# Two small scale tables share one tile, and a pin on the second projection stays for the first tile only

## The chip, the cores and the metric

The kernel runs on one core of a Trainium2 chip. The metric is the device time of one execution in microseconds (us). The five engines are called PE (TensorE, matmuls; its weight loads are listed apart as PEld), DVE (VectorE), ACT (ScalarE), POOL (GpSimd) and SP (SyncE, which here only issues DMAs). Each has its own queue of instructions and works it off in order; they wait for one another with semaphores.

## The reference

Two layers of a decoder trunk over 1024 positions of width 1024, all in float32. A layer normalises its input, projects it once to 1312 columns, and gives the columns to three mixers: attention over a sliding window of 128, a pooling mixer, and latent attention over all earlier positions. The mixers' outputs go through one output projection and are added to the residual stream; then comes a gated feed-forward part of inner width 2816.

```
for l in range(DEPTH):
    h = rms_norm(x, attn_norm[l])
    proj = h @ w_in[l]
    ...
    mixed = jnp.concatenate([out_a, out_b, out_c], axis=-1)
    x = x + mixed @ w_out[l]
    h = rms_norm(x, ffn_norm[l])
    x = x + (jax.nn.silu(h @ w_gate[l]) * (h @ w_up[l])) @ w_down[l]
```

## The kernel before, in words

**Numbers.** Every matmul operand is split into two parts, `hi` (rounded to the matmul's type) and `lo` (the rest), with a copy on ACT and a subtraction on DVE (`split`, L57 and L58). A product is then three matmuls: hi with hi, hi with lo, lo with hi. They are the triples of lines L445 to L447, L879 to L881, L1079 to L1081 and L1232 to L1234. In `te.matmul(acc, a, b)` the second argument is the stationary tile (128 columns, loaded as weights), the third the moving one (512 columns wide in most cases).

**Stages.** For each layer: `phase1` (projection, sliding window, pooling), `phase2` (latent attention, output projection), and `phase34`, which is the feed-forward part: `gate_up` and then `down`.

- `phase1` loops over 8 tiles of 128 positions. Per tile, `group0` projects to the first 512 columns (weights `wa` against the transposed input `hT`), then come `proj(512, 512)` (weights `wb`) and `proj(1024, 288)`. Each has 8 triples. What comes out is evacuated on ACT, scaled, and goes into attention. A scheduler puts the instructions of all engines in order by a modelled timeline when the program is built; `tc.issue_after(i)` holds it from placing the instructions in its block before instruction `i`. `G["mm"]` is the last matmul that `proj` made. So the line `with tc.issue_after(G["mm"].ins): acc = proj(512, 512)` pins the second projection of every tile behind the last matmul of the first.
- `gate_up` works on the weights in 44 stages in all (2 layers, 11 pairs of inner columns, gate and up). A stage is a product of 2 x 2 blocks with 7 block products instead of 8. Each block product (`prod`, L1228) is 4 triples, 12 matmuls, so a stage has 84. Moving tiles are the seven blocks of the transposed input, `T1` to `T4`, `B11`, `B21`, `B22`, which stay for the whole stage; stationary are the weights, split into tiles `A11`, `A12` and `sb`. The sums of blocks are made on POOL. Results of a pair are multiplied, split into `go` and stored to DRAM (`gd`).
- `down` does the same for the last projection in 4 chunks of 7 products (L1079 to L1081): stationary is `ga`, loaded from `gd`, moving is `op`, split from the loaded weights `rw`. 1848 matmuls in both layers.

**Memory.** Tiles are placed by pools on two stacks, one that grows up from the low end (left, the default) and one that grows down from the high end (`side="right"`). The first pool of the left stack, `cst`, holds small constants and the residual `xm`, and what is allocated later stands on top of it. Each tile takes a multiple of 32 bytes per partition. In `gate_up`, `T2`, `T3`, the weights as loaded (`raw4`), `A11`, `A12`, `sb` and part of `go` are on the left; `T1`, `T4`, `B11`, `B21`, `B22` are on the right. In `down`, `ga`, the accumulators and the weights of chunks 2 to 4 (`rw`) are on the left, `op` and the first chunk's `rw` on the right.

The start of each tile, in bytes modulo 512, as the program before is built (the parts of a tile that one matmul reads lie multiples of 512 bytes apart, so they start alike):

| part | left stack | right stack |
|---|---|---|
| gate_up | T2, T3, raw4, A11, A12, sb, left go: 0 | T1, T4, B11, B21, B22, right go: 480 |
| down | ga, rw of chunks 2 to 4: 0 | op, rw of chunk 1: 480 |
| phase 1 | hT: 480; wa: 96; wb: 480, 352, 224 or 96 | |
| output projection | moving 0, 128 or 256 on stationary 256; moving 128 on 128 | |

The tables of the change, `gq` and `gm`, are scale vectors of two columns. `gq` is read at L483 and L484 (scale of the queries), `gm` is written in `Boot.bias` and read in phase 2.

Of the kernel before, what the change touches and what calls it, by code (L numbers as in the profile page):

```python
# [11 lines left out]
F32 = mybir.dt.float32  # L12
# [9 lines left out]
P = 128  # L22
# [7 lines left out]
DEPTH = 2  # L30
# [5 lines left out]
@with_exitstack  # L36
def trunk(ctx: ExitStack, tc: tile.TileContext, A, out):
    nc = tc.nc
    ve, sc, gp, te, sy = nc.vector, nc.scalar, nc.gpsimd, nc.tensor, nc.sync

    def pool(stack, name, bufs=1, space=None, side=None):
        kw = {}
        if space is not None:
            kw["space"] = space
        if side is not None:
            kw["side"] = side
        if space != DRAM:
            kw["reuse_waits"] = "tile"
        return stack.enter_context(tc.tile_pool(name=name, bufs=bufs, **kw))

    def gap(stack, name, n, side=None):
        nc.gpsimd.memset(pool(stack, name, side=side).tile([P, n // 4], F32, name="gap")[:, 0:1], 0.0)

    def f(ap):
        return ap.bitcast(F32)

    def split(hi, lo, src):  # L57
        return sc.copy(hi, src), ve.tensor_tensor(out=lo, in0=src, in1=f(hi), op=ALU.subtract)  # L58

    def mm3(dst, terms, first=True, last=True):  # L60
        n = len(terms)
        for i, (a, b) in enumerate(terms):
            te.matmul(dst, a, b, start=first and i == 0, stop=last and i == n - 1)

    def bcast(row, n):
        return row.unsqueeze(0).to_broadcast([P, n])


    cst = pool(ctx, "cst")
    dram = pool(ctx, "dram", space=DRAM)  # L70

    ident = cst.tile([P, P], F32, name="ident")
    nhalf = cst.tile([P, 32], F32, name="nhalf")
    gp.memset(nhalf, -0.5)
    cmask = cst.tile([P, P], F32R, name="cmask")
    identr = cst.tile([P, P], F32R, name="identr")
    invc = cst.tile([P, 2, 16], F32, name="invc")
    sinks = cst.tile([P, DEPTH, 6], F32, name="sinks")
    gna = cst.tile([P, DEPTH * KT], F32, name="gna")
    gqk = cst.tile([P, 4], F32, name="gqk")  # L80
    gains = cst.tile([P, 14], F32, name="gains")
    pscale = gains[:, 0:4].rearrange("p (l k) -> p l k", l=DEPTH)
    gc = [[gains[:, 4 + 2 * l : 5 + 2 * l], gains[:, 5 + 2 * l : 6 + 2 * l], gains[:, 8 + l : 9 + l]] for l in range(DEPTH)]
    gq = cst.tile([P, DEPTH], F32, name="gq")
    gm = cst.tile([P, DEPTH], F32, name="gm")
    cosT = cst.tile([P, NT, 16], F32, name="cosT")
    sinT = cst.tile([P, NT, 16], F32, name="sinT")
    krr = cst.tile([P, NT, 32], F32, name="krr")
    rc = cst.tile([P, NT, 2], F32, name="rc")
    g32 = [cst.tile([P, 32], F32, name=f"g32{l}") for l in range(DEPTH)]  # L90
    rn = cst.tile([P, NT], F32, name="rn")
    xm = cst.tile([P, NT, KT, P], F32, name="xm")
    xrow = [xm[:, t].rearrange("p k c -> p (k c)") for t in range(NT)]

    xres = dram.tile([S, D], F32, name="xres")
    xp = [[dram.tile([P, D], F32, name=f"xp{l}{t}") for t in range(NT)] for l in range(DEPTH)]
    bias_keep = dram.tile([P, 6, 256], F32, name="biask")


    for l in range(DEPTH):  # L100
        xsrc = A["x"][0] if l == 0 else xres
        G = dict(
            ident=ident, xm=xm, xrow=xrow, krr=krr, rc=rc, cosT=cosT, sinT=sinT, sinks=sinks,
            pscale=pscale, invc=invc, nhalf=nhalf, gq=gq, gm=gm, cmask=cmask, identr=identr, rn=rn, gc=gc, g32=g32, xsrc=xsrc, dram=dram, gap=gap, xp=xp, gns=ExitStack(), bias_keep=bias_keep)
        G["gna"], G["gains"], G["gqk"] = gna, gains, gqk
        phase1(nc, tc, A, l, pool, split, f, bcast, G)
        phase2(nc, tc, A, l, pool, split, f, bcast, G)
        phase34(nc, tc, A, l, pool, split, f, bcast, G, xres, out)
# [217 lines left out]
def phase1(nc, tc, A, l, pool, split, f, bcast, G):  # L326
# [3 lines left out]
    with ExitStack() as ph:  # L330
# [104 lines left out]
        for t in range(NT):  # L435
# [5 lines left out]
            def proj(c0, n, hT=hT):  # L441
                acc = ps_mm.tile([P, 512], F32, name="acc")
                for k in range(KT):
                    hi, lo = wcol(0, k, c0, n), wcol(1, k, c0, n)
                    te.matmul(acc[:, 0:n], hT[:, 0, k], hi, start=k == 0, stop=False)  # L445
                    te.matmul(acc[:, 0:n], hT[:, 0, k], lo, start=False, stop=False)  # L446
                    G["mm"] = te.matmul(acc[:, 0:n], hT[:, 1, k], hi, start=False, stop=k == KT - 1)  # L447
                return acc
# [3 lines left out]
            def group0(t):  # L452
                acc = proj(0, 512, hTs[t])
                qk = evq.tile([P, 512], F32, name="qk")
                behind.append(sc.activation(qk, acc, AF.Copy, scale=rows[t]))
                sq = evq.tile([P, 8, 64], F32, name="sq")
                sc.activation(sq.rearrange("p a b -> p (a b)"), qk, AF.Square, scale=0.125)
                ms8 = three.tile([P, 8], F32, name="ms8")
                ve.tensor_reduce(ms8, sq, AX.X, ALU.add)
                return qk, rstd_of(nc, ms8, 8, G["nhalf"])  # L460
# [34 lines left out]

            if l == 0 and t == 0:
                ahead[1] = group0(1)
            with tc.issue_after(G["mm"].ins):
                acc = proj(512, 512)
            vt = three.tile([P, 2, 2, 64], F32R, name="vt")  # L500
            vsrc = acc[:, 0:128].rearrange("p (g d) -> p g d", g=2)
# [476 lines left out]
def phase34(nc, tc, A, l, pool, split, f, bcast, G, xres, out):  # L978
    ve, sc, gp, te, sy = nc.vector, nc.scalar, nc.gpsimd, nc.tensor, nc.sync
    ident, xm, xrow, xp = G["ident"], G["xm"], G["xrow"], G["xp"][l]  # L980
    last = l == DEPTH - 1
    HB = S // 2
    HK = KT // 2
    gd = [[G["dram"].tile([P, 2, HB], F32, name=f"gd{l}_{i}_{p}") for p in range(7)] for i in range(NF // 2)]

    with ExitStack() as ph:
        ps_gu = pool(ph, f"p4gu_{l}", bufs=5, space=PSUM)
        ps_d = pool(ph, f"p4dn_{l}", bufs=3, space=PSUM)
        gate_up(nc, tc, A, l, pool, split, f, bcast, G, ps_gu, ps_d, gd)
        G["gns"].close()  # L990

        down(nc, tc, A, l, pool, split, f, G, (ps_gu, ps_d), gd, xres, out)
# [391 lines left out]
```

## Time and profile before

| | us |
|---|---|
| median of three runs | 2220.33 (2215.66 to 2223.3) |
| the profiled execution | 2220.96 |
| its span in the trace | 2219.2 |
| PE busy in the span | 2142.4 |
| DVE busy | 1690.1 |
| ACT busy | 1088.0 |
| POOL busy | 979.7 |

By the timeline, layer 0 is in phase 1 until about 185 us, in phase 2 until about 440, in gate_up until 888 and in down until 1107; layer 1 follows with 1108, 1291, 1543 and 1996, and ends at 2214. The phases overlap somewhat at their edges.

How to read the rows: a group of the page reads line, engine, operation, out<-in, shapes and count, then busy time and the mean of one in ns, then the engine's idle time before these instructions and who ended it. Matmuls overlap, so what one costs is the distance between two starts on the timeline (start, duration, engine, line, operation). A window's row has the busy time of each engine in it, the granted clock of PE, the share of time that the DMA engines are busy, and GB/s.

### The profile page before, as it was taken

What the parts mean: (1) busy time and instruction counts of PE and PEld (TensorE: products, weight loads), DVE (VectorE), ACT (ScalarE), POOL (GpSimd) and SP (SyncE); (2) the same over time, 40 slices, a digit from 0 to 9 for tenths busy, and PEclk for the clock granted to TensorE, in tenths of its full rate; (3) what the DMA queues carried; (4) which work ended last, traced back from release to release, by engine and by line L of the source; (5) the groups of instructions that cost most, each with busy time, mean ns of one, the idle gap of its engine ahead of it and who ended that gap; (6) DMA issues with size and microseconds to landing.
All of it is one profiled execution on the core that took longest, in us unless ns stands there. A gap on an engine that the chain in (4) does not pass through costs nothing.

```text
span 2219.2 us, 29675 instructions
## 1 busy us (share of the span) xinstructions
PE 2142.4 (97%) x10423; PEld 1766.2 (80%) x10423; DVE 1690.1 (76%) x2595; ACT 1088.0 (49%) x2301; POOL 979.7 (44%) x916
## 2 busy tenths in 40 slices
PE   8998999999999999999989989999999999999999
PEld 6886888877888888788778868888778888887887
DVE  6667888799887887765745688888988878877657
ACT  7777676563434333311356776666534343333111
POOL 2434455255454442621623455452554544436215
PEclk9999999999999999999999999999999999999999
DMA  6003211424434345965520032113244344359754
GB/s 210 1 1 109 83 59 46 134 69 161 166 131 158 136 149 211 417 262 194 200 79 1 1 107 79 67 43 135 76 153 164 138 152 144 143 217 415 265 192 161
DMA packets 133732, 312.16 MB, mean 141 GB/s; under 512 B 13071, under 2 KB 63952, under 8 KB 133584
## 3 DMA queue, kind: packets, MB, share of 16 engines
q1 hardware_dynamic: 133396, 310.19, 38.8%
q8 instruction: 83, 1.36, 0.2%
q14 instruction: 65, 0.53, 0.1%
q10 hardware_dynamic: 188, 0.08, 0.0%
HBM read 203.53 MB, written 106.70 MB: 140 GB/s over the span
## 4 chain that ended last, share of the span: by engine, by line
PE 77%; DVE 9%; DMA 5%; ACT 4%; POOL 3%; issue 2%; SPq 0%; DVEq 0%; POOLq 0%; ACTq 0%
PE gu L1232 11%; PE gu L1234 11%; PE gu L1233 11%; PE dn L1079 6%; PE dn L1080 6%; PE dn L1081 6%; PE acc L445 3%; PE acc L447 3%; PE acc L446 3%; PE tp L840 2%; DMA rw<-in_w_down_dram 2%; PE po L881 1%; PE po L880 1%; PE po L879 1%; PE ss L816 1%
## 5 line engine op out<-in xcount | busy, mean ns | idle before, releaser
L1234 PE MATMUL gu<-T,sb 128*128 128x512 f32 x704 | 277.9, 395 | 6.4 <-DVE sb L58 6.3
L1232 PE MATMUL gu<-T,sb 128*128 128x512 f32 x704 | 278.9, 396 | 3.1 <-ACT sb L58 1.5
L1233 PE MATMUL gu<-T,sb 128*128 128x512 f32 x704 | 278.2, 395 | 0.0
L1079 PE MATMUL dn<-op,ga 128*128 128x512 f32 x616 | 243.7, 397 | 4.8 <-DMA ga<-gd 4.8
L1080 PE MATMUL dn<-op,ga 128*128 128x512 f32 x616 | 244.2, 396 | 0.0
L1081 PE MATMUL dn<-op,ga 128*128 128x512 f32 x616 | 243.4, 396 | 0.0
L1028 POOL TENSOR_TENSOR rw<-rw 128x1536 f32<-128x1536 f32 (+1 forms) x32 | 113.0, 3543 | 254.8 <-DVE op L1038 162.5
L58 ACT CAST go<-xm 128x512 fp32r<-128x512 f32 x154 | 95.2, 620 | 265.2 <-POOL xm L1266 91.5
L1037 ACT CAST op<-rw 128x1536 fp32r<-128x1536 f32 (+1 forms) x56 | 76.7, 1373 | 280.7 <-PE dn L1081 273.1
L1209 POOL TENSOR_TENSOR xm<-raw 128x512 f32<-128x512 f32 x44 | 69.0, 1569 | 324.7 <-DMA raw<-in_w_up_dram 155.1
L58 DVE TENSOR_TENSOR go<-xm,go 128x512 fp32r<-128x512 f32 x154 | 152.9, 1002 | 40.8 <-ACT go L58 37.0
L58 ACT CAST sb<-raw 128x512 fp32r<-128x512 f32 x180 | 110.4, 617 | 133.4 <-PE gu L1234 111.6
L1234 PEld LDWEIGHTS gu<-T,sb 128*128 128x128 f32 x704 | 132.9, 189 | 39.8 <-DVE sb L58 9.3
L1232 PEld LDWEIGHTS gu<-T,sb 128*128 128x128 f32 x704 | 132.8, 189 | 36.6 <-ACT sb L58 3.3
L58 DVE TENSOR_TENSOR sb<-raw,sb 128x512 fp32r<-128x512 f32 x180 | 157.3, 875 | 1.3 <-ACT sb L58 0.3
L1233 PEld LDWEIGHTS gu<-T,sb 128*128 128x128 f32 x704 | 132.9, 189 | 30.2
L1266 POOL TENSOR_TENSOR xm<-xm 128x512 f32<-128x512 f32 x88 | 141.6, 1617 | 31.0 <-DVE go L58 19.6
L1079 PEld LDWEIGHTS dn<-op,ga 128*128 128x128 f32 x616 | 116.1, 188 | 33.7 <-ACT op L1037 5.6
L1038 DVE TENSOR_TENSOR op<-rw,op 128x1536 fp32r<-128x1536 f32 (+1 forms) x56 | 112.0, 2000 | 39.4 <-ACT op L1037 37.1
L1080 PEld LDWEIGHTS dn<-op,ga 128*128 128x128 f32 x616 | 116.2, 189 | 28.1
L1081 PEld LDWEIGHTS dn<-op,ga 128*128 128x128 f32 x616 | 116.2, 189 | 28.0
L1232 PE MATMUL gu<-B,A 128*128 128x512 f32 x336 | 134.5, 400 | 2.8 <-ACT B L58 2.3
(332 smaller groups left out, 6106.1 us busy)
## 6 DMA issues: line engine op xcount, KB each, us to landing
gd<-go SPq DMA_DIRECT2D x154, 512.0 KB, 3.1
ga<-gd SPq DMA_DIRECT2D x154, 512.0 KB, 5.7
raw<-in_w_gate_dram SPq DMA_DIRECT2D x22, 1024.0 KB, 5.4
raw<-in_w_up_dram SPq DMA_DIRECT2D x22, 1024.0 KB, 6.1
rw<-in_w_down_dram SPq DMA_DIRECT2D x44, 512.0 KB, 8.2
xp<-xt SPq DMA_DIRECT2D x32, 256.0 KB, 2.0
old<-xp SPq DMA_DIRECT2D x16, 512.0 KB, 4.2
xp<-xm SPq DMA_DIRECT2D x16, 512.0 KB, 2.9
```

The lines of the kernel that those rows point to most:

```text
L58: return sc.copy(hi, src), ve.tensor_tensor(out=lo, in0=src, in1=f(hi), op=ALU.subtract)
L1028: gp.tensor_tensor(out=o, in0=a, in1=b, op=ALU.subtract)
L1037: sc.copy(t[:, 0], q[b])
L1038: ve.tensor_tensor(out=t[:, 1], in0=q[b], in1=f(t[:, 0]), op=ALU.subtract)
L1079: te.matmul(acc, S_[:, j, 0, ts], T_[:, 0, j], start=j == 0, stop=False)
L1080: te.matmul(acc, S_[:, j, 0, ts], T_[:, 1, j], start=False, stop=False)
L1081: te.matmul(acc, S_[:, j, 1, ts], T_[:, 0, j], start=False, stop=j == h - 1)
L1209: gp.tensor_tensor(out=s1, in0=q["A21"], in1=q["A22"], op=ALU.add)
L1232: te.matmul(acc, s[:, 0, k], b[:, 0, k], start=k == 0, stop=False)
L1233: te.matmul(acc, s[:, 0, k], b[:, 1, k], start=False, stop=False)
L1234: te.matmul(acc, s[:, 1, k], b[:, 0, k], start=False, stop=k == HK - 1)
L1266: gp.tensor_tensor(out=q[o], in0=q[a], in1=q[b], op=op)
```

## The change

Two edits. The two tables become the halves of one tile, so `cst` has one tile less. And the pin on the second projection is kept for the first tile of layer 0 only; for the other 15 tiles the scheduler may place that projection's matmuls where it likes.

```diff
-    gq = cst.tile([P, DEPTH], F32, name="gq")
-    gm = cst.tile([P, DEPTH], F32, name="gm")
+    gqm = cst.tile([P, 2 * DEPTH], F32, name="gqm")
+    gq, gm = gqm[:, 0:DEPTH], gqm[:, DEPTH : 2 * DEPTH]
...
-            with tc.issue_after(G["mm"].ins):
+            with tc.issue_after(G["mm"].ins) if l == 0 and t == 0 else nullcontext():
                 acc = proj(512, 512)
```

The first edit takes one slot of 32 bytes out of the left stack. Everything allocated behind it on the left moves down by 32 bytes per partition; the right stack stays. Modulo 512, the left tiles of gate_up and down go from 0 to 480, so that in both all moving and all stationary tiles start at 480. In phases 1 and 2 all these tiles are on the left, and those of a matmul move together (hT to 448, wa to 64, wb to 448, 320, 192 or 64); the identity matrix, allocated ahead of the tables, stays at 128.

The second edit changes the order of instructions in phase 1 and, in its wake, at the beginning of phase 2. In gate_up and down PE has the same order as before; on SP a few loads and stores of down change places.

The first place is PE in layer 0, tile 2, with `wa` the weights of the first projection and `wb` those of the second. Before, where the first projection ends:

```order
L445 MATMUL acc<-wa_193,hT 128x512
L446 MATMUL acc<-wa_201,hT 128x512
L447 MATMUL acc<-wa_193,hT 128x512
L445 MATMUL acc<-wb_170,hT 128x512
L446 MATMUL acc<-wb_178,hT 128x512
L447 MATMUL acc<-wb_170,hT 128x512
```

After, from the second projection's fourth triple on (buffer numbers are one lower, since there is one tile less):

```order
L445 MATMUL acc<-wb_172,hT 128x512
L446 MATMUL acc<-wb_180,hT 128x512
L447 MATMUL acc<-wb_172,hT 128x512
L445 MATMUL acc<-wa_189,hT 128x512
L446 MATMUL acc<-wa_197,hT 128x512
L445 MATMUL acc<-wb_173,hT 128x512
L446 MATMUL acc<-wb_181,hT 128x512
L447 MATMUL acc<-wa_189,hT 128x512
```

Before, all 24 matmuls of the first projection stand ahead of the second. After, 12 of them do, then 12 of the second follow, and then the two mix: 14 matmuls of the second projection now stand ahead of the last one of the first.

The second place is PE in layer 1, tile 0, where the second projection (512 wide) begins and the third (288 wide) is next. Before:

```order
L445 MATMUL acc<-wb_10684,hT 128x512
L446 MATMUL acc<-wb_10692,hT 128x512
L447 MATMUL acc<-wb_10684,hT 128x512
L445 MATMUL acc<-wb_10685,hT 128x512
L446 MATMUL acc<-wb_10693,hT 128x512
L447 MATMUL acc<-wb_10685,hT 128x512
```

After, from the second triple on:

```order
L445 MATMUL acc<-wb_10684,hT 128x512
L446 MATMUL acc<-wb_10692,hT 128x512
L447 MATMUL acc<-wb_10684,hT 128x512
L445 MATMUL acc<-wb_10683,hT 128x288
L446 MATMUL acc<-wb_10691,hT 128x288
L447 MATMUL acc<-wb_10683,hT 128x288
```

Before, the second projection runs through all its eight triples ahead of the third. After, the third starts behind two triples of the second, and from there they take turns.

## The prediction

> **What bounds the kernel now.** I read the page first, then windows of busy time by stage, then the timeline of TensorE (PE) inside one feed-forward stage.
>
> ```profile
> span 2219.2 us, 29675 instructions
> PE 2142.4 (97%) x10423; PEld 1766.2 (80%) x10423; DVE 1690.1 (76%) x2595; ACT 1088.0 (49%) x2301; POOL 979.7 (44%) x916
> PE 77%; DVE 9%; DMA 5%; ACT 4%; POOL 3%; issue 2%; SPq 0%; DVEq 0%; POOLq 0%; ACTq 0%
> L1234 PE MATMUL gu<-T,sb 128*128 128x512 f32 x704 | 277.9, 395 | 6.4 <-DVE sb L58 6.3
> L1079 PE MATMUL dn<-op,ga 128*128 128x512 f32 x616 | 243.7, 397 | 4.8 <-DMA ga<-gd 4.8
> ```
>
> PE is busy for 97% and carries 77% of the chain that ended last. Its mean per matmul (395 ns) overlaps the next matmul, so the cost of one is the distance between two starts. The windows (us, busy time of PE, weight load, DVE, ACT, POOL, then granted clock, DMA share, GB/s) show where PE is full:
>
> ```profile
> 0.00:185.00 185.00, 170.40 (x941) 143.84 (x942) 118.12 (x262) 139.05 (x367) 60.91 (x153) 0.98 0.25 80
> 442.00:500.00 58.00, 54.13 (x242) 42.51 (x241) 54.49 (x73) 35.23 (x65) 33.19 (x24) 0.97 0.23 75
> 500.00:880.00 380.00, 378.04 (x1623) 305.68 (x1622) 312.87 (x382) 150.72 (x261) 177.07 (x113) 1.00 0.43 153
> 1543.00:1600.00 57.00, 53.23 (x255) 41.52 (x255) 51.18 (x75) 39.51 (x75) 26.49 (x20) 1.00 0.29 95
> ```
>
> From 500 to 880 us PE is busy for 378.04 of 380 and DVE for 312.87: only a faster matmul shortens this. Whether one can be faster is seen in one stage, the start of the first matmul of each block of 12 (T2, T1, T3, B22, T4, B11, B21, and T2 of the next stage), with two rows inside the first:
>
> ```profile
> 620.42 0.39 PE L1232 MATMUL gu<-T,sb 128*128 128x512 f32 x1
> 621.58 0.39 PE L1234 MATMUL gu<-T,sb 128*128 128x512 f32 x1
> 622.94 0.39 PE L1234 MATMUL gu<-T,sb 128*128 128x512 f32 x1
> 623.16 0.40 PE L1232 MATMUL gu<-T,sb 128*128 128x512 f32 x1
> 625.97 0.39 PE L1232 MATMUL gu<-T,sb 128*128 128x512 f32 x1
> 628.71 0.40 PE L1232 MATMUL gu<-B,sb 128*128 128x512 f32 x1
> 631.51 0.40 PE L1232 MATMUL gu<-T,sb 128*128 128x512 f32 x1
> 634.31 0.40 PE L1232 MATMUL gu<-B,A 128*128 128x512 f32 x1
> 637.11 0.40 PE L1232 MATMUL gu<-B,A 128*128 128x512 f32 x1
> 639.91 0.39 PE L1232 MATMUL gu<-T,sb 128*128 128x512 f32 x1
> ```
>
> The blocks with T2 and T3 as moving tile take 2.74 us (620.42 to 623.16, 625.97 to 628.71), the other five 2.80 or 2.81. Inside T2 the first five steps take 1.16 us (232 ns each, still the slow pace), the six from 621.58 to 622.94 take 1.36 (226.7 ns each). The same instruction with the same stationary tile settles at 226.7 or stays at 2.80/12 = 233.3. T2 and T3 are the two moving tiles that lie in the left stack, at 0 modulo 512, where the stationary tiles lie too; the other five lie in the right stack, at 480.
>
> **The change, part by part.**
>
> *The shared tile.* No instruction goes; the readers of gq and gm wait for what they waited for. Everything behind the tile on the left moves down by 32 bytes: T2, T3 and all stationary tiles of gate_up and down go from 0 to 480, the right stack stays at 480. So every pair in the feed-forward part agrees. The price of agreement is 226.7 ns a matmul if address is the cause. Two places outside test that: in the output projection the moving tile lies at 0 for the matmuls from 439.30 and at 128 for those from 440.43, the stationary one at 256.
>
> ```profile
> 439.30 0.39 PE L880 MATMUL ss<-wot,ch 128*128 128x512 f32 x1
> 440.43 0.40 PE L879 MATMUL ss<-wot,ch 128*128 128x512 f32 x1
> 441.12 0.49 PE L1155 MATMUL tp<-ident,xm 128*128 128x128 f32 x3
> ```
>
> Five steps at (0, 256) take 1.13 us, 226 each; three at (128, 256) take 0.69, 230 each. In phase 1 the pair is (480, 480) for the three matmuls on the first wb tile (the start of the fourth closes them):
>
> ```profile
> 96.81 0.39 PE L445 MATMUL acc<-wb,hT 128*128 128x512 f32 x1
> 97.50 0.40 PE L445 MATMUL acc<-wb,hT 128*128 128x512 f32 x1
> 1227.31 0.39 PE L445 MATMUL acc<-wb,hT 128*128 128x512 f32 x1
> 1227.76 0.39 PE L447 MATMUL acc<-wb,hT 128*128 128x512 f32 x1
> 1227.99 0.40 PE L445 MATMUL acc<-wb,hT 128*128 128x512 f32 x1
> ```
>
> They take 0.69 and 0.68 us, and the last step of the second set 0.23 (1227.76 to 1227.99): compatible with 226.7, too short a run to settle. I read the rows as: what counts is that the two starts agree modulo 256.
>
> Gate_up: a stage of 84 matmuls takes 639.91 − 620.42 = 19.49 us; at 226.7 throughout, 19.04. That is 0.45 us; 2 layers x 11 x (gate, up) = 44 stages give **−19.8**. Down has 3 x 616 = 1848 matmuls (the L1079 row and its two sisters), all at 480 against 0:
>
> ```profile
> 957.65 0.40 PE L1079 MATMUL dn<-op,ga 128*128 128x512 f32 x1
> 964.65 0.40 PE L1079 MATMUL dn<-op,ga 128*128 128x512 f32 x1
> ```
>
> 30 steps in 7.00 us are 233.3 each; 1848 x 6.6 ns is **−12.2**. Together −32.0.
>
> The Trainium skill speaks against this in "SBUF — State Buffer", section "Who interferes with whom": PE reads the moving tile and the weights through two independent ports, so the relation of their addresses should cost nothing, and these 32.0 would be 0. The trace disagrees, 2.74 against 2.80 us for equal blocks.
>
> What takes some back: at the entry of each feed-forward part DVE, not PE, sets the pace (54.49 busy of 58, 51.18 of 57). There a faster PE only waits longer: (242 + 255) matmuls x 5.4 ns (0.45/84) = **+2.7**.
>
> *The hand-over to down.* Here transfers bind. The window, the DMA view of 880 to 945 us and the row of the wait:
>
> ```profile
> 888.00:940.00 52.00, 49.65 (x207) 39.61 (x206) 37.72 (x33) 18.93 (x26) 30.82 (x13) 0.97 1.03 417
> GB/s 406 418 408 424 424 416 424 416 413 401 368 418 421 406 418 429 411 426 418 413 429 413 426 418 418 421 418 426 413 426 418 413 431 398 426 418 416 424 416 426
> ga<-gd SPq DMA_DIRECT2D x23, 512.0 KB, 9.9
> 918.24 0.47 PE L1079 MATMUL dn<-op,ga 128*128 128x512 f32 x1 [2.35 <-DMA ga<-gd]
> ```
>
> At 918.24 PE has waited 2.35 us for ga; the group's 4.8 for the whole run says that layer 1 has as long a wait. Transfers are full (share 1.03), so a PE that comes sooner waits longer: 918.24 − 888 is 30 us, 30/0.2333 x 6.6 ns = 0.8 us a layer that isn't won. Second, ga, the left half of go and the later weights now land at 480 instead of 0 modulo 512. No row prices that: the mean of 417 already mixes tiles at both places. Bounds: nothing (rate as now), or the lowest slice, 368, over the 38 us of full transfers that the view shows before the wait (880 to 918): 38 x (417/368 − 1) = 5.1. I take the lower of the ordinary slices, 406: 38 x (417/406 − 1) = 1.0, since most slices lie within 3% although tiles at 480 are among them. So 1.8 a layer, **+3.6** (bounds 1.6 to 11.8). On SP's queue in down one store of go, one reload of the residual rows and three loads of weights change places with a few ga loads, all behind the wait at 918, and each layer takes roughly the order that the other has now; as both wait 2.4, I cost it at nothing, and were that cover gone it is one ga landing more, 9.9 us at full queues, inside the range's upper end for one layer. The Trainium skill bears on it in "DMA: Bandwidth & Descriptors", section "How a descriptor splits into AXI transactions": an access that does not start on a 256-byte boundary fetches from the boundary below. A 4096-byte row at 480 starts 224 past one and would take 135 beats for 128, an estimate of 5.5% or 2.1 us a layer in place of 1.0; no run here shows it yet.
>
> *The order in phase 1.* Without the pin, the second projection of most tiles mixes with the first, or the third. With the matmuls move their evacuations on ACT and DVE and the small power instructions on POOL; no DMA is issued by them. Nothing is added; whom it serves changes. PE waits there for this:
>
> ```profile
> PE acc L445 <- ACT hT L58: 6.2, 6, 1.4
> PE tp L616 <- DVE pT L58: 5.9, 1, 5.9
> ```
>
> (1108 to 1291 us, and 0 to 185.) At best the 6.2 us for hT are filled; at worst the first projection ends 14 matmuls later (3.3 us) before its qk chain, and one more wait like the 5.9 opens. PE idles for 14.6 us of the first window, so later work has cover in both directions: I take **0** (−6.2 to +5.9).
>
> The profiled execution took 2220.96 us (span 2219.2 and 1.8 around it), 0.6 above the median of 2220.33, so I use its own time. Sum: 2220.96 − 32.0 + 2.7 + 3.6 + 0 = 2195.3, **2195 us**.
>
> **Rivals.**
>
> *Half of it.* Agreement buys the faster pace only where a block has settled, and the steady change of stationary tiles, or DVE's casts, unsettles it again. For: the five slow steps at the start of T2. Against: those follow a block that disagrees, and 226.7 then holds across six weight loads. Half of the gain: 2220.96 − 16.0 + 1.4 + 3.6 = 2210.
>
> *The addresses are not the cause, but the ends of the memory.* Fast blocks have both tiles in the left stack, slow ones one on each side. Then nothing changes in the feed-forward part, and only slower landings remain: 2220.96 + 2 x 1.0 = 2223. The rule of the Trainium skill's "SBUF — State Buffer" above, that the two reads never meet, would give this too. Against: the wa tiles (96) and hT (480) are both on the left, and still
>
> ```profile
> 68.33 0.40 PE L445 MATMUL acc<-wa,hT 128*128 128x512 f32 x1
> 70.42 0.28 PE L597 MATMUL s<-kr,qs 128*128 128x256 f32 x1
> ```
>
> nine of them take 2.09 us, 232 each.
>
> *Slower: a moving tile at 480 is slow by itself.* All 4488 matmuls that stay at 233.3 (5 blocks x 12 x 44, and 1848 of down) have their moving tile at 480; the settled runs shown have it at 0. Then T2 and T3 lose what they have: 2 blocks in each of 44 stages, 2.80 − 2.74 = 0.06 us a block, +5.3; the other blocks and down gain nothing, and landings add 2.0: 2220.96 + 7.3 = 2228, with the upper bound of landings (2 x 5.1) 2236. It decides as soon as a T2 block takes over 2.78 us. For: no long run at (480, 480) exists in this trace. Against: the two triples at 1227 and 97 us, and the (128, 256) matmuls, which a good place of the moving tile alone would let settle.
>
> **How the numbers follow.** Forecast 0.76; half 0.08; nothing 0.05; slower 0.11. The forecast's own range is 2184 (no loss at the entries, transfers at 1.6, phase 1 at −6.2) to 2204 (transfers at 11.8). The half case at 2210 is taken in: 2184 to 2212 leaves out the last two cases, 0.16, and little more. About 0.3% (6.7 us) is what a measurement of this kernel can tell from no change. Faster: 0.76 and most of the half case, 0.83. Same: nothing, and the edges of half and slower, 0.07. Slower: 0.10.
>
> **What would show it.** Right: all seven blocks of a stage at 2.72 us, a stage at 19.04 to 19.1; 30 steps of down in 6.80; the wait for ga at the hand-over grown from 2.35 to about 4.2; DVE's share in gate_up up by some 2%. Wrong: T2 blocks at 2.80 (slower), T1 blocks still at 2.80 (nothing), blocks between 2.75 and 2.78 (half); a wait for ga over 8.3 us (2.35 + 5.9) (landings dearer than my bound); PE's idle time before 185 us or between 1108 and 1291 moved by over 6 us (the order mattered).

## The result, and the profile after

The changed kernel takes 2192.48 us (median of 4 runs, 2191.64 to 2196.21) against 2221.55 for the kernel before (4 runs): ratio 0.9877, 95% interval 0.9855 to 0.9899, so about 27 us or 1.2% faster (the two medians lie 29 apart). The profiled execution took 2191.85 us, its span 2190.0, 29.2 less than the span before. Run again with the last experiments the ratio was 0.9878 (0.9858 to 0.9899).

The page of the changed kernel:

```profile
span 2190.0 us, 29669 instructions
PE 2106.4 (96%) x10423; PEld 1762.0 (80%) x10423; DVE 1696.8 (77%) x2595; ACT 1083.7 (49%) x2301; POOL 972.0 (44%) x916
L1234 PE MATMUL gu<-T,sb 128*128 128x512 f32 x704 | 276.1, 393 | 7.5 <-DVE sb L58 7.4
L1079 PE MATMUL dn<-op,ga 128*128 128x512 f32 x616 | 240.5, 392 | 8.1 <-DMA ga<-gd 6.9
```

The count of matmuls is the same, PE's busy time is 36 us less. The waits behind it grew: for `sb` from 6.3 to 7.4 us, for `ga` from 4.8 to 6.9. Note how little the mean of one (393 against 395 ns) shows: it contains the overlap with the next matmul. The starts show the change. One stage of gate_up, the first matmul of each block (T2, T1, T3, B22, T4, B11, B21, next T2):

```profile
617.48 0.39 PE L1232 MATMUL gu<-T,sb 128*128 128x512 f32 x1
620.20 0.39 PE L1232 MATMUL gu<-T,sb 128*128 128x512 f32 x1
622.92 0.39 PE L1232 MATMUL gu<-T,sb 128*128 128x512 f32 x1
625.64 0.39 PE L1232 MATMUL gu<-B,sb 128*128 128x512 f32 x1
628.36 0.39 PE L1232 MATMUL gu<-T,sb 128*128 128x512 f32 x1
631.08 0.39 PE L1232 MATMUL gu<-B,A 128*128 128x512 f32 x1
633.80 0.39 PE L1232 MATMUL gu<-B,A 128*128 128x512 f32 x1
636.52 0.39 PE L1232 MATMUL gu<-T,sb 128*128 128x512 f32 x1
```

Every block takes 2.72 us, the stage 19.04 instead of 19.49, as forecast. In down, 34 steps between two starts of the same line take 7.71 us, 226.8 ns each:

```profile
950.13 0.39 PE L1079 MATMUL dn<-op,ga 128*128 128x512 f32 x1
957.84 0.39 PE L1079 MATMUL dn<-op,ga 128*128 128x512 f32 x1
```

Two windows of the changed kernel, the entry of the first feed-forward part and its steady stretch:

```profile
442.00:500.00 58.00, 53.39 (x242) 42.46 (x241) 54.24 (x72) 34.38 (x64) 33.21 (x24) 0.97 0.23 75
500.00:880.00 380.00, 377.48 (x1655) 311.17 (x1654) 324.10 (x387) 151.43 (x264) 178.38 (x113) 1.00 0.45 160
```

In the first, PE issues 242 matmuls in 58 us, as many as before: there the faster step gains nothing, DVE (54.24 busy) sets the pace, as the prediction had it. In the second it issues 1655 instead of 1623, 2.0% more in the same time, and DVE's busy time rises with it (312.87 to 324.10).

Where the time went, by the start of PE's first instruction of each phase (us, from the timeline; gate_up begins with its first transpose, L1155, and the last column ends with the last matmul's start):

| kernel | layer 0: phases 1, 2 | gate_up | down | layer 1: phases 1, 2 | gate_up | down |
|---|---|---|---|---|---|---|
| before | 429.5 | 453.5 | 222.1 | 433.2 | 453.2 | 218.1 |
| after | 428.5 | 446.1 | 218.8 | 427.1 | 444.8 | 214.8 |
| after, run again | 431.8 | 446.3 | 218.7 | 424.3 | 445.6 | 215.4 |

Before to after (unrounded), gate_up gives 15.7 us, down 6.7, phases 1 and 2 give 7.2, of which 6.2 in layer 1.

These times scatter between executions of one kernel, and the traces show one reason. The granted clock of PE is either full or one half, and the halves come in pieces of 3.41 us, or two or three in a row. At half clock equal matmuls start 427 ns apart (rows below), so a piece in which PE is busy costs 1.7 us. Layer 1's phases 1 and 2 had 30.7 us at half clock in one profile of the changed kernel, 20.5 in the other and 27.3 in the profile before. Where the text says "at full clock", half of such time is taken off: an estimate, since PE is not busy throughout.

### The profile page after: what moved, and what is told of

Same layout as the page of the kernel before. It is cut to its first block, busy times and chain, and to the rows that moved or that the text cites. A ratio compares the mean times of both kernels' runs of the same rounds, so it can differ in the third digit from the quotient of the medians.

```text
span 2190.0 us, 29669 instructions
## 1 busy us (share of the span) xinstructions
PE 2106.4 (96%) x10423; PEld 1762.0 (80%) x10423; DVE 1696.8 (77%) x2595; ACT 1083.7 (49%) x2301; POOL 972.0 (44%) x916
## 3 DMA queue, kind: packets, MB, share of 16 engines
q8 instruction: 83, 1.36, 0.3%
## 4 chain that ended last, share of the span: by engine, by line
PE 48%; DVE 6%; DMA 4%; ACT 2%; issue 1%; POOL 1%; SPq 0%; DVEq 0%; ACTq 0%; POOLq 0%
PE gu L1234 6%; PE gu L1233 6%; PE gu L1232 6%; PE dn L1079 5%; PE dn L1081 5%; PE dn L1080 5%; PE acc L445 2%; PE acc L446 2%; PE acc L447 2%; DMA ga<-gd 1%; PE tp L840 1%; DMA raw<-in_w_up_dram 1%; PE po L881 1%; PE po L879 1%; DVE xm L1069 1%
## 5 line engine op out<-in xcount | busy, mean ns | idle before, releaser
L1079 PE MATMUL dn<-op,ga 128*128 128x512 f32 x616 | 240.5, 392 | 8.1 <-DMA ga<-gd 6.9
L1080 PE MATMUL dn<-op,ga 128*128 128x512 f32 x616 | 240.7, 391 | 0.0
L1081 PE MATMUL dn<-op,ga 128*128 128x512 f32 x616 | 240.0, 391 | 0.0
```

The lines of the kernel that those rows point to most:

```text
L1079: te.matmul(acc, S_[:, j, 0, ts], T_[:, 0, j], start=j == 0, stop=False)
L1080: te.matmul(acc, S_[:, j, 0, ts], T_[:, 1, j], start=False, stop=False)
L1081: te.matmul(acc, S_[:, j, 1, ts], T_[:, 0, j], start=False, stop=j == h - 1)
```

## The experiments

The theory after the result: the shared tile gives about 22 us, all in the feed-forward part, because moving and stationary tiles then agree modulo 256 bytes; the new order gives about 7 us in phase 1. Rivals: everything comes from the addresses (phase 1 moved by 32 bytes as well); agreement modulo 512 is needed; it matters at which place the tiles lie; landings at 480 cost transfers. Each kernel was timed against the kernel before on the same chip.

**The shared tile alone.**

```diff
-            with tc.issue_after(G["mm"].ins) if l == 0 and t == 0 else nullcontext():
+            with tc.issue_after(G["mm"].ins):
```

(against the changed kernel)

> The shared tile alone, with the pin on the second projection of every tile as before; each engine has the order of the kernel before. Theory (address and order add up): the feed-forward part takes what it takes after, 22.4 us less than before (gate_up 440.0 + 438.7 against 447.4 + 447.1 us between PE's starts, down 218.8 + 214.8 against 222.1 + 218.1), and phases 1 and 2 what they took before, so 2221 - 22 = 2199 us. Rival (the 7 us that phases 1 and 2 lost come from their tiles lying 32 bytes lower, not from the order): all of the change is in this edit, 2192 us.

(It counts gate_up from a start 6 us later than the table.) Measured: 2196.01 us against 2218.75, ratio 0.9902 (0.9885 to 0.9920), so 22 us; the rival's 29 would be 0.987. In its profile gate_up and down give 13.5 and 5.0 us, and phases 1 and 2 are 6.9 us shorter too. At full clock, though, phases 1 and 2 take 837 us here as before, and the feed-forward part 22 us less: the lower addresses do nothing in phases 1 and 2 that can be told.

**The new order alone**, with the tables apart, so against the kernel before:

```diff
-            with tc.issue_after(G["mm"].ins):
+            with tc.issue_after(G["mm"].ins) if l == 0 and t == 0 else nullcontext():
```

> The pin kept for the first tile only, with gq and gm as two tiles; each engine has the order of the kernel after, the addresses are those before. Theory: feed-forward blocks as before (five of seven at 2.80 us), phases 1 and 2 shorter by 7 us, so 2214 us. Rival (the order is worth nothing, as forecast): 2221 us.

Measured: 2211.59 us, ratio 0.9968 (0.9956 to 0.9981). The two parts add up: 0.9902 x 0.9968 = 0.9870, beside 0.9877 and 0.9878 for the whole. So the addresses are worth 22 us, the order 7 (interval 4 to 10), and the forecast's "order 0" fell.

**Which agreement?** Three kernels with the order of the kernel before, differing in padding only. Left stack at 224, right at 480:

```diff
-    gm = cst.tile([P, DEPTH], F32, name="gm")
+    gm = cst.tile([P, DEPTH], F32, name="gm"); gp.memset(cst.tile([P, 56], F32, name="pad")[:, 0:1], 0.0)
```

> As before, with 224 bytes of padding in the constants: the left stack of the feed-forward part starts at 224 modulo 512, the right one stays at 480. They agree modulo 256 and disagree modulo 512. Theory of the forecast (agreement modulo 256 is enough): all seven blocks at 2.72 us, the run like the shared tile alone, about 2199 us. Rival (agreement modulo 512 is needed, as the words of the change have it): five blocks of seven at 2.80 us, 2221 us.

Measured: 2193.11 us, ratio 0.988 (0.9859 to 0.9900). The start of a T2 block, of the T1 block and of the T3 block in it:

```profile
614.25 0.39 PE L1232 MATMUL gu<-T,sb 128*128 128x512 f32 x1
616.97 0.39 PE L1232 MATMUL gu<-T,sb 128*128 128x512 f32 x1
619.69 0.39 PE L1232 MATMUL gu<-T,sb 128*128 128x512 f32 x1
```

T2 (224 on 224) and T1 (480 on 224) both take 2.72 us: 256 bytes apart is as good as the same place. The same padding with 88 columns puts the left stack at 352, 128 from the right one:

```diff
-    gm = cst.tile([P, DEPTH], F32, name="gm")
+    gm = cst.tile([P, DEPTH], F32, name="gm"); gp.memset(cst.tile([P, 88], F32, name="pad")[:, 0:1], 0.0)
```

> As before, with 352 bytes of padding in the constants: left stack at 352 modulo 512, right stack at 480, so 128 apart, every engine in the order of the kernel before. Theory (agreement modulo 256 is what counts): the five blocks with a moving tile on the right stay at 2.80 us, T2 and T3 at 2.74, the run as before, 2219 us. Rival (agreement modulo 128 is enough, or any padding helps): seven blocks at 2.72 us, 2195 us. A third case, blocks between 2.74 and 2.79, would mean that the distance sets the price.

Measured: 2216.10 us against 2218.86, ratio 0.9991 (0.9981 to 1.0001): as before. Its T2, T1 and T3 blocks, and the start of the next:

```profile
600.04 0.39 PE L1232 MATMUL gu<-T,sb 128*128 128x512 f32 x1
602.77 0.40 PE L1232 MATMUL gu<-T,sb 128*128 128x512 f32 x1
605.56 0.39 PE L1232 MATMUL gu<-T,sb 128*128 128x512 f32 x1
608.30 0.40 PE L1232 MATMUL gu<-B,sb 128*128 128x512 f32 x1
```

T2 takes 2.73 us (352 on 352), T1 2.79 (480 on 352), T3 2.74. T2 and T3 stay at the faster pace although they moved, T1 at the slower one: among these places only the distance of a tile from the other counts, and 128 is not enough. The third moves the right stack to 0, where the left one lies:

```diff
-    gp.memset(nhalf, -0.5)
+    gp.memset(nhalf, -0.5); gp.memset(pool(ctx, "padr", side="right").tile([P, 120], F32, name="pad")[:, 0:1], 0.0)
```

> As before, with 480 bytes of padding at the high end: the right stack of the feed-forward part moves to 0 modulo 512, where the left one lies. Theory (only the relation counts for PE): seven blocks at 2.72 us, as with both at 480. Landings: if tiles at 480 cost the transfers at the hand-over the 1 us a layer of the forecast, the waits for ga are that much shorter than in the kernel after (3.4 us a layer), and the run is 2 us below the shared tile alone, 2197 us; if the place of landing costs nothing, 2199 us and waits of 3.4 us. Rival (a moving tile must not start at 0 on the right, or any other place matters): blocks over 2.75 us.

Measured: 2195.44 us, ratio 0.9892 (0.9876 to 0.9908), beside 0.9902 with both at 480: no difference that can be told. Its blocks are at 2.72 us:

```profile
613.76 0.39 PE L1232 MATMUL gu<-T,sb 128*128 128x512 f32 x1
616.48 0.39 PE L1232 MATMUL gu<-T,sb 128*128 128x512 f32 x1
619.20 0.39 PE L1232 MATMUL gu<-T,sb 128*128 128x512 f32 x1
```

What it tells of landings is in three windows of 50 us that begin 8 us ahead of down's first matmul in layer 0; the last figure is GB/s. Before (left at 0, right at 480):

```profile
879.70:929.70 50.00, 47.65 (x199) 38.02 (x198) 39.94 (x34) 19.70 (x27) 28.62 (x12) 0.97 1.03 416
```

after (all at 480):

```profile
871.70:921.70 50.00, 45.62 (x193) 36.95 (x192) 38.72 (x31) 19.66 (x27) 28.70 (x12) 0.97 1.03 412
```

and with all at 0:

```profile
867.70:917.70 50.00, 45.92 (x195) 37.23 (x194) 39.20 (x32) 19.77 (x27) 28.68 (x12) 0.97 1.03 419
```

So full transfers were about 1% slower with all tiles at 480 (416 to 412; in layer 1 414 to 411), and all at 0 gives 419 and 413. The left stack at 224 or 352 gave 411 or 412 as well, so it is not 480 as such. But PE's waits for `ga` were not shorter with all at 0:

```profile
PE dn L1079 <- DMA ga<-gd: 8.4, 4, 3.0
```

That is 8.4 us, against 6.9 after. The place of landing alone did not set those waits, and that part of the expectation fell. (With the left stack at 352 and the pace as before they were 6.6, against 4.8 to 5.8 in the five profiles with the addresses of before; a small part for the landing is not ruled out.)

**Where the order gains.** Three kernels with the addresses of before. The pin for all of layer 0, none in layer 1:

```diff
-            with tc.issue_after(G["mm"].ins):
+            with tc.issue_after(G["mm"].ins) if l == 0 else nullcontext():
```

> Addresses as before; the pin kept for all tiles of layer 0 and dropped in layer 1, so that only layer 1's phase 1 has another order. Theory (the order wins 3.7 us in phase 1 of each layer, where PE no longer waits for the transposed input): phase 1 of layer 1 at 189 us between PE's starts instead of 193, the run 2215 us. Rival (the gain is all layer 0's, or comes from the order of phase 2 that follows it): 2219 us.

Measured: 2211.63 us, ratio 0.9967 (0.9955 to 0.9980): all 7 us, not half. Layer 0 free but for its first tile, layer 1 pinned:

```diff
-            with tc.issue_after(G["mm"].ins):
+            with tc.issue_after(G["mm"].ins) if l == 1 or t == 0 else nullcontext():
```

> Addresses as before; the pin dropped in layer 0 but for its first tile, and kept for all tiles of layer 1. The scheduler's order then differs from the changed one in a few rows of layer 1 alone. Theory (3.7 us a layer): if the pin itself is what costs in layer 1, half of the gain is left, 2215 us; if layer 1's order is set by how layer 0 ended in the scheduler's model, nearly all of it, 2212 us. Rival (the gain is all layer 1's): 2219 us.

Measured: 2212.56 us, ratio 0.9971 (0.9961 to 0.9981). Both halves give the whole gain, so "3.7 us a layer" fell, and the case came true that layer 1's order follows from how layer 0 ended. And no pin for any tile:

```diff
-            with tc.issue_after(G["mm"].ins):
+            with nullcontext():
```

> Addresses as before; no pin for any tile, the first of layer 0 included. Theory (the first tile's pin keeps matmuls whose weights have not come yet out of PE's way): PE waits for wb in the first 50 us, some 3 us more, 2215 us. Rival (the exception for the first tile is worth nothing): 2212 us, as with the pin on the first tile.

Measured: 2209.34 us, ratio 0.9955 (0.9941 to 0.9968): not slower, so the first tile's pin guards nothing that can be measured. The phases of one profile each (us, as in the table above):

| kernel | order of phase 1 | layer 0: phases 1, 2 | layer 1: phases 1, 2 |
|---|---|---|---|
| before; tile alone; left 224; both 0; left 352 | pinned | 429.5; 427.2; 424.7; 425.0; 428.3 | 433.2; 428.6; 429.1; 434.5; 428.7 |
| after; again; order alone | first tile pinned | 428.5; 431.8; 431.7 | 427.1; 424.3; 423.2 |
| layer 0 freed | layer 0 as after, layer 1 nearly so | 428.9 | 420.8 |
| layer 1 freed | layer 0 pinned | 428.6 | 424.9 |
| no pin | free | 425.9 | 427.4 |

In layer 1 every new order lies below every pinned one (420.8 to 427.4 against 428.6 to 434.5); at full clock these are 411.7 to 415.7 against 416.8 to 419.6, some 4 to 5 us. In layer 0 nothing is gained (425.9 without a pin and 428.5 to 431.8 otherwise, against 424.7 to 429.5). The kernel with layer 1 pinned still gains there, because the scheduler chose nearly the changed order for layer 1, a consequence of what it had placed in layer 0. It is the order that counts, not the pin as such. What PE no longer waits for in layer 1 is `hT`: in the wait list of phase 1 it stood at 6.2 us in six waits before. With layer 1 freed:

```profile
PE po L620 <- DVE xm L624: 2.7, 1, 2.7
...
PE acc L445 <- ACT hT L58: 0.7, 1, 0.7
```

and in the changed kernel:

```profile
PE po L879 <- ACT wo L58: 4.5, 1, 4.5
...
PE acc L445 <- ACT hT L58: 0.7, 1, 0.7
```

5.5 us of these waits are gone; the second list shows a new one at the start of phase 2, for the output weights. That the 5.5 us are the 7 is not shown: no run removed that wait alone, and others came in its place. PE's whole idle time in phases 1 and 2 of layer 1 was 26.6 us before and 21.7 with layer 1 freed, but 24.6 in the changed kernel and 25.3 with the order alone. The rest of the gain lies in PE's busy time, and its cause stays open.

**Put together.** Three kernels beside the changed one, which ran again:

> The changed kernel once more, beside the three below. Theory (address -22 us and order -7 us add up): ratio to the kernel before 0.987, about 2190 us where that one takes 2219.

Measured: 2191.83 us against 2219.98. The changed kernel without its last pin:

```diff
-            with tc.issue_after(G["mm"].ins) if l == 0 and t == 0 else nullcontext():
+            with nullcontext():
```

> The changed kernel without its last pin: the shared tile, and no pin for any tile. Theory (the parts add up): 22 us for the addresses and 9.5 us for the order without pins, 2219 - 31.5 = 2187 us, 2 to 3 us faster than the changed kernel. Rival (the first tile's pin is neutral, and the 2 us between the two orders were chance): 2190 us.

Measured: 2186.39 us, ratio 0.9864 (0.9839 to 0.9888): near the theory's 2187, but the rival's 2190 lies in the interval too. The pin kept for all of layer 0, none in layer 1:

```diff
-            with tc.issue_after(G["mm"].ins) if l == 0 and t == 0 else nullcontext():
+            with tc.issue_after(G["mm"].ins) if l == 0 else nullcontext():
```

> The shared tile, the pin kept for all tiles of layer 0 and dropped in layer 1. Theory (the order's gain arises in layer 1 alone, where PE waited for hT): as the changed kernel, 2190 us. Rival (layer 0 has a part in it): 3 us or more slower than the changed kernel.

Measured: 2185.69 us, ratio 0.9854 (0.9829 to 0.9879). Its runs (2183.70 to 2189.21) lie almost wholly below those of the changed kernel (2188.35 to 2193.86), its phases 1 and 2 take 426.9 and 423.2 us. By medians it is 6 us below the changed kernel, and 0.7 below the one without a pin; the intervals of the ratios overlap. The runs had different clocks, too (the table at the end of this section). Last, the rule in phase 1: padding of 128 bytes ahead of `wa`, in the kernel without a pin:

```diff
-        wt = pool(ph, f"p1t_{l}")
+        gap(ph, f"p1u_{l}", 128); wt = pool(ph, f"p1t_{l}")
```

> As the one without any pin, with 128 bytes of padding ahead of the weights of the first projection, so that wa and hT also agree modulo 256 (192 and 192; wb agree as often as before). Theory (agreement modulo 256 counts for every matmul 512 wide): the 384 matmuls on wa settle at 227 ns instead of 232 where they run in a row, 2 us less at most, 2185 us. Rival (phase 1 has other bounds, PE's gain is lost in waits): time as without the padding, though the steps are at 227. Against both: the steps stay at 232.

Measured: 2190.46 us, ratio 0.9873 (0.9852 to 0.9893), no gain. Fifteen steps on `wa` without the padding (64 on 448), then with it (192 on 448):

```profile
111.07 0.40 PE L445 MATMUL acc<-wa,hT 128*128 128x512 f32 x1
114.58 0.39 PE L445 MATMUL acc<-wa,hT 128*128 128x512 f32 x1
```

```profile
111.06 0.39 PE L445 MATMUL acc<-wa,hT 128*128 128x512 f32 x1
114.45 0.39 PE L445 MATMUL acc<-wa,hT 128*128 128x512 f32 x1
```

3.51 us against 3.39, 234 against 226 ns a step: the rule holds here too. That phase 1 waits for others often enough to swallow 2 us is argued; so small a gain can't be told in four runs.

**Which differences are the clock's?** Every run's span and mean granted clock are on record. Their product estimates the span at full clock; the means, less that of the kernel before in the same session, have standard errors of 1 to 2 us:

| kernel | clock (kernel before) | at full clock, us |
|---|---|---|
| tile alone; left 224; both 0 | 0.9875; 0.9900; 0.9880 (0.9880) | −22.9; −22.2; −24.1 |
| left 352 | 0.9875 (0.9877) | −2.4 |
| order alone | 0.9882 (0.9880) | −6.9 |
| layer 1 freed; layer 0 freed; no pin | 0.9880; 0.9871; 0.9898 (0.9877) | −6.7; −7.7; −5.5 |
| after, again | 0.9868 (0.9883) | −29.9 |
| shared tile and no pin; pin in layer 0 alone; no pin and `wa` padded | 0.9885; 0.9898; 0.9870 (0.9883) | −29.3; −28.7; −30.6 |

The 22 and the 7 us stay. What the last four kernels seemed to gain on one another goes with their clocks: none of them is shown to be better than the changed kernel.

## Why the prediction was right or wrong

**Agreement: right, and its reading sharpened.** 227 ns a step for every pair that agrees modulo 256, at 480, at 0, and at 480 on 224; the 128-apart kernel is the control. Distances of 0, 32 and 128 modulo 256 were run, no others. The agreement modulo 512 that the change aims at is more than is needed. This holds against the rule of the Trainium skill, "SBUF — State Buffer", section "Who interferes with whom", by which the two reads of PE cannot disturb each other; 0.45 us a stage says that the relation of their addresses costs something in this layout. That the two reads meet somewhere is one way to explain it; no run shows what meets. All three rivals fell with the first stage of the trace, where T1 and the other blocks with a moving tile on the right take 2.72 us.

**Gate_up: −17.1 forecast with the entry, −15.7 measured**, −13.5 with the shared tile alone (448.1 and 445.1 us). The settled pace was right to the digit, and the entry gave nothing, as argued from DVE. The term that was too large is the pace over all 44 stages: outside PE's waits and at full clock the 3696 matmuls of gate_up took 17.9 us less, not 19.8 (233.2 to 228.4 ns a step on average, where the forecast took the settled stage's 232.0 to 226.7). PE's waits grew by 2.3 us where 2.7 were forecast; with the shared tile alone they grew by 4.3.

**Down: −8.6 forecast with the hand-over, −6.7 measured.** The pace gave 12.0 us of the 12.2. The waits came out in size: PE's idle time in down is the length of a row less its first busy time. Before, layer 0 and layer 1:

```profile
887.73:1109.88 222.15, 217.54 (x926) 174.50 (x924) 148.01 (x160) 57.40 (x63) 94.68 (x47) 0.99 0.70 268
1996.31:2214.38 218.07, 215.60 (x925) 173.43 (x923) 143.51 (x150) 45.52 (x44) 87.88 (x35) 1.00 0.68 260
```

and after:

```profile
879.66:1098.42 218.76, 211.78 (x925) 174.25 (x924) 151.44 (x161) 56.95 (x63) 93.16 (x47) 0.99 0.73 273
1970.31:2185.08 214.77, 211.09 (x924) 174.08 (x923) 145.04 (x151) 45.83 (x44) 89.21 (x35) 0.99 0.68 262
```

7.1 us became 10.7, and the 3.6 more are the forecast's 3.6: the waits for `ga` grew by 2.1, and a new one for `op` came. What the sum left out stands behind the wait, where PE's steps nearly doubled. The changed kernel at the hand-over of layer 0, and PE's clock there (0.50 in the window's row):

```profile
902.72 0.47 PE L1079 MATMUL dn<-op,ga 128*128 128x512 f32 x1 [1.14 <-ACT op L1037]
...
911.68 0.47 PE L1079 MATMUL dn<-op,ga 128*128 128x512 f32 x1 [3.24 <-DMA ga<-gd]
...
912.63 0.63 PE L1079 MATMUL dn<-op,ga 128*128 128x512 f32 x1
...
915.19 0.60 PE L1079 MATMUL dn<-op,ga 128*128 128x512 f32 x1
```

```profile
912.20:915.60 3.40, 3.40 (x9) 2.63 (x8) 0.00 (x0) 0.00 (x0) 0.00 (x0) 0.50 1.03 416
```

Six steps from 912.63 to 915.19 take 427 ns each. Down has one such piece before (layer 0) and two after (both layers): 1.7 us more, nearly all that is missing. That the term of the waits was right in size is in part luck, for its second half had the wrong cause. I had charged 1.0 us a layer to slower landings by taking the slice of 406 GB/s; the measured 416 to 412 is 0.4 us over the same 38, and the kernel with all at 0 saved none of the waits. The estimate by the Trainium skill, "DMA: Bandwidth & Descriptors", section "How a descriptor splits into AXI transactions", 5.5%, is further off: 412 against 419 is 1.7%. Why `ga` comes later, counted from the start of down (918.24 − 887.7 = 30.5 us before, 911.68 − 879.7 = 32.0 after), is not settled.

**Order: 0 forecast, −7 measured.** This step failed. I had set "waits for hT filled" as the best end (−6.2) and took 0 because PE's idle time seemed to give cover both ways. But a wait of PE is no cover when PE is what ends last there. The runs put the gain into layer 1, where the six waits for hT stood; how much of it they are is open (above). The sign that the prediction named for it, PE's idle time moved by over 6 us, would have missed it: before 185 us it hardly moved, and in the stretch from 1108 to 1291 it went from 15.9 to 13.5 (1097 to 1272 after).

Sum: −25.7 forecast, −29 measured. (The upper end of the forecast's own range, 2204, leaves out its +5.9 for the order; with it the end is 2209.) The total was near because a feed-forward part that won 3 us less met an order that won 7 more; that the two nearly cancel is luck.

## What to carry to other kernels

Where PE is full, measure the distance between starts of equal matmuls block by block, and sort it by the addresses of the two operands: two paces in one trace are a gain that costs only padding. Here agreement modulo 256 was enough, and 32 bytes of a constant decided it for 4488 matmuls; print the addresses, since any small tile can undo it. When a pin on the scheduler goes, time the order by itself: here it was worth 7 us that PE's idle time as a whole did not announce. And before kernels a few us apart are ranked, compare the clocks that their runs were granted.

## What was not expected of the hardware

- With the operands 128 apart, single steps alternate (in a block of the kernel with the left stack at 352 mostly 229 and 238 ns) and their mean is 232 to 233; at 32 apart they lie between 231 and 235. Both cost the same.
- Full transfers ran at 412 GB/s with all tiles at 480 modulo 512, 419 with all at 0 and 416 with a mixture (layer 0; 411, 413 and 414 in layer 1).
- A wait of PE of 3.24 us was followed by half clock to 915.6 on the timeline. Before, a wait of 2.35 us in layer 0 was followed by it too, one of 2.47 us in layer 1 was not. The traces show how these two differ. The clock changes only on a grid of 3.41 us. Ahead of the half clock at 919.61, PE was busy for 1.36 us of one such window; the other wait fell across two windows, with 2.37 and 1.97 us busy:

```profile
916.20:919.60 3.40, 1.36 (x6) 1.17 (x7) 2.17 (x2) 1.20 (x1) 0.53 (x1) 1.00 1.03 420
919.61:923.02 3.41, 3.41 (x10) 2.63 (x9) 0.00 (x0) 0.00 (x0) 0.00 (x0) 0.50 1.03 420
2022.10:2025.50 3.40, 2.37 (x11) 1.56 (x9) 2.75 (x4) 1.00 (x1) 3.32 (x1) 1.00 1.03 423
2025.50:2028.90 3.40, 1.97 (x9) 1.63 (x10) 1.76 (x1) 0.47 (x1) 0.00 (x0) 1.00 1.02 419
```
